# Around each inner LayerNorm: a hand-written order on four engines, transposes among the output matmuls, next weights split ahead, a ring of six

## The chip, the cores and the metric

The kernel runs on one core of a Trainium2 chip. Its time is the device time of one launch in microseconds (us); the kernel before takes 1643.83 us, the median of three runs (1643.48 to 1646.4). Five engines work side by side, each on its own list of instructions: TensorE (PE) multiplies, VectorE (DVE) and ScalarE (ACT) work element by element, GpSimd (POOL) does a few small things, and SyncE (SP) issues the weight transfers. They wait for each other by semaphores.

## What is computed

Two layers on 256 tokens of width 1024. In each, with a = 4^(1/4):

```
x <- LN1(a*x + 1/2 * (silu(x Wg) * (x Wu)) Wo)      first FFN, inner width 4096
x <- LN2(a*x + M(x))                                 the mixer
x <- LN3(a*x + 1/2 * (silu(x Wg') * (x Wu')) Wo')    second FFN
```

M(x) projects x once, runs three mixers on parts of it (gated DeltaNet, chunk attention with a relative bias, sliding-window attention with sinks), projects each back to 1024, weights the three with sigmoid gates of x, adds them (the merge), and multiplies by an output matrix. LN is a LayerNorm over the 1024 channels with gain and bias. All is float32.

## The kernel before

The 256 tokens are two row tiles of 128, called t = 0 and t = 1. Every product is done in three matmuls on split operands: a weight `raw` becomes `hi` (a rounded copy, by ACT, L90) and `lo` (raw minus hi, by DVE or POOL, L91); the activations x are split the same way into `xhl` (hi by ACT at L142, lo by DVE at L144). Then hi·hi, hi·lo and lo·hi are summed in PSUM. Weights come in chunks of 1 MB through SP's queue into three `raw` buffers; the halves go into rings of five `hi` and five `lo` buffers, and some chunks into other tiles that are free at the time.

An FFN runs over 32 column units u. Unit u multiplies x by one chunk (gate and up columns), and the output matrix is added up in blocks of two units. The last six units' output matmuls are done by `finish` (L222), row tile by row tile, and behind each row tile comes `norm` (L311): per half of 512 channels, x plus the PSUM sum (L317) and its statistics (L318), then mean and variance (L320, L322), the reciprocal root on POOL (L324), times gain (L326), plus bias (L335). Then PE transposes the eight 128x128 blocks of the row tile (L338) into PSUM, and ACT and DVE split them into `xhl` in two groups of four (L142, L144). The first three units of an FFN that follows a LayerNorm, and the first projection of the mixer (324 columns, twice), are multiplied with x as the stationary operand, so that row tile 0 can start before row tile 1 is normalized (L301 to L303, and `rows`, L220); the gated rows of those three units are transposed one by one (L270).

The mixer starts with four chunks of that first projection, then goes through a fixed list of projections, gates and branches (ORDER). Branches end with a merge on DVE (L602, L605), a split of the merged tiles (L142, L146), the output matrix through `finish`, and LN2. In the branches and the output matrix the program puts part of the `lo` splits on POOL; so it does for four of the six splits of an FFN's first three units (PFF).

The order of instructions on each engine is worked out before the run by a scheduler that simulates the program (`schedule_with_timeline_sim=True`), not by the order in the source. Weight transfers leave SP in the order in which the scheduler puts them. LayerNorm gains and biases are loaded through POOL's queue (`load_ln`), those of the first FFN of layer 0 through SP's.

There are six LayerNorms: LN1, LN2 and LN3 in each layer. The last one only writes the result. In the profiled execution LN1 of layer 0 lies at about 255 to 292 us from the span's start, LN2 at 532 to 578 and LN3 at 812 to 850; in layer 1 LN1 lies at 1070 to 1108 and LN2 at 1348 to 1394.

## Time and profile before

| | |
|---|---|
| median of three runs | 1643.83 us |
| the profiled execution | 1646.21 us, of which the span 1644.5 us |
| mean granted TensorE clock | 0.997 |
| PE busy | 1620.9 us |
| DVE / ACT / POOL busy | 1045.7 / 791.5 / 175.3 us |
| PE waiting, as the list of waits has it | for the merge 3.4 us, for mixer scores 3.1 us, for split x 1.5 + 1.1 + 0.8 us |

The table is read from the slowest (here the only) core. Busy time of PE is modelled from the starts of pipelined matmuls: the record of a 256-column matmul reads 0.28 us, though the next starts 0.12 us after it, so gaps are read from starts, and durations of PE records are not added up.

### The profile page before, as it was taken

To read this page: it belongs to the slowest core of one execution; us is meant where nothing else is said; L and a number is where in the kernel's file an instruction comes from. 1 tells how busy PE (TensorE), PEld (TensorE's weight loads), DVE (VectorE), ACT (ScalarE), POOL (GpSimd) and SP (SyncE) were. 2 spreads that over 40 slices of the span, in tenths; PEclk is the share of its full clock that TensorE was granted. 3 is DMA by queue.
4 is the path that set the end of the run, shared out by engine and by line. 5 is a ranking of instruction groups with operands and counts; after the bars stand their busy time and mean duration, and the time that the engine had idled before them with its cause. 6 is when DMAs were issued, how large, how long until landed. Compare 5 with 4: busy or idle time off the path is not lost.

```text
span 1644.5 us, 29265 instructions
## 1 busy us (share of the span) xinstructions
PE 1620.9 (99%) x12238; PEld 1511.0 (92%) x12238; DVE 1045.7 (64%) x1580; ACT 791.5 (48%) x1297; POOL 175.3 (11%) x145
## 2 busy tenths in 40 slices
PE   8999999999999999999999999999999999999998
PEld 7999998999889899999899999989988889999997
DVE  6555556889669755555655555667986696555555
ACT  5444453665444444444444444536744444544442
POOL 0000002123014400000110000011320053000000
PEclk9999999999999999999999999999999999999999
DMA  8655553634335555555555555535353355555552
GB/s 295 248 203 184 202 208 113 226 138 156 129 127 198 182 204 183 203 184 201 186 198 184 201 187 198 209 140 203 134 167 118 108 191 193 206 185 199 187 198 78
DMA packets 52341, 298.28 MB, mean 181 GB/s; under 512 B 11600, under 2 KB 13520, under 8 KB 18672
## 3 DMA queue, kind: packets, MB, share of 16 engines
q1 hardware_dynamic: 50208, 289.39, 49.2%
q0 software_dynamic: 2000, 7.01, 1.3%
q8 instruction: 96, 1.57, 0.4%
q14 instruction: 37, 0.30, 0.1%
HBM read 294.94 MB, written 1.44 MB: 180 GB/s over the span
## 4 chain that ended last, share of the span: by engine, by line
PE 93%; DVE 4%; ACT 1%; DMA 1%; issue 0%; SPq 0%; POOL 0%; DVEq 0%; ACTq 0%; POOLq 0%
PE mm L189 37%; PE sm L189 20%; PE acc L204 16%; PE acc L220 8%; DVE lo L91 2%; PE acc L192 1%; PE acc L301 1%; PE acc L303 1%; PE acc L685 1%; PE sm L515 1%; PE acc L302 1%; PE sm L566 1%; PE sm L507 1%; PE sm L514 1%; ACT hi L90 1%; DVE cv L459 1%
## 5 line engine op out<-in xcount | busy, mean ns | idle before, releaser
L91 DVE TENSOR_TENSOR lo<-raw,hi 128x1024 fp32r<-128x1024 f32 (+1 forms) x498 | 617.3, 1245 | 470.6 <-ACT hi L90 469.9
L90 ACT ACTIVATE hi<-raw 128x1024 fp32r<-128x1024 f32 (+1 forms) x542 | 564.2, 1050 | 645.9 <-PE mm L189 196.9
L189 PE MATMUL mm<-xhl,hi 128*128 128x256 f32 x3488 | 618.1, 280 | 0.0
L189 PEld LDWEIGHTS mm<-xhl,hi 128*128 128x128 f32 x3488 | 533.2, 189 | 8.9 <-issue 5.8
L189 PE MATMUL mm<-xhl,lo 128*128 128x256 f32 x1744 | 486.5, 279 | 0.0
L189 PE MATMUL sm<-xhl,hi 128*128 128x256 f32 x1952 | 338.7, 277 | 0.8 <-ACT hi L90 0.8
L189 PEld LDWEIGHTS mm<-xhl,lo 128*128 128x128 f32 x1744 | 329.6, 189 | 4.3 <-issue 2.4
L189 PEld LDWEIGHTS sm<-xhl,hi 128*128 128x128 f32 x1952 | 296.1, 188 | 3.0 <-ACT hi L90 1.0
L189 PE MATMUL sm<-xhl,lo 128*128 128x256 f32 x976 | 270.0, 277 | 0.8 <-DVE lo L91 0.8
L204 PE MATMUL acc<-hi,g 128*128 128x512 f32 x728 | 200.4, 391 | 0.0
L189 PEld LDWEIGHTS sm<-xhl,lo 128*128 128x128 f32 x976 | 183.4, 188 | 2.0 <-DVE lo L91 1.0
L204 PEld LDWEIGHTS acc<-hi,g 128*128 128x128 f32 x728 | 132.4, 188 | 24.2
L91 POOL TENSOR_TENSOR lo<-raw,hi 128x1024 fp32r<-128x1024 f32 (+1 forms) x44 | 104.0, 2377 | 367.5 <-DVE g L144 241.2
L204 PE MATMUL acc<-lo,g 128*128 128x512 f32 x416 | 128.4, 390 | 0.0
L204 PEld LDWEIGHTS acc<-lo,g 128*128 128x128 f32 x416 | 78.1, 188 | 16.8
L324 POOL TENSOR_TENSOR rs<-ve,nh 128x1 f32<-128x1 f32 x12 | 11.8, 985 | 764.6 <-DVE ve L322 764.6
L220 PE MATMUL acc<-hi,g 128*128 128x512 f32 x320 | 92.8, 392 | 0.0
L220 PEld LDWEIGHTS acc<-hi,g 128*128 128x128 f32 x320 | 59.3, 188 | 13.3 <-ACT g L142 0.8
L220 PE MATMUL acc<-lo,g 128*128 128x512 f32 x160 | 54.7, 391 | 0.0
L144 DVE TENSOR_TENSOR g<-th,g 128x256 fp32r<-128x256 f32 x119 | 51.0, 429 | 2.1 <-ACT g L142 1.9
L142 ACT ACTIVATE g<-th 128x256 fp32r<-128x256 f32 x119 | 47.7, 401 | 6.4 <-DVE th L243 6.4
L459 DVE SCALAR_TENSOR_TENSOR cv<-cin,par,cv 128x256 f32<-128x256 f32 x72 | 41.7, 624 | 0.2
(231 smaller groups left out, 1538.2 us busy)
## 6 DMA issues: line engine op xcount, KB each, us to landing
raw<-w2i SPq DMA_DIRECT2D x64, 1024.0 KB, 4.8
raw<-w1i SPq DMA_DIRECT2D x62, 1024.0 KB, 4.8
raw<-w1o SPq DMA_DIRECT2D x32, 1024.0 KB, 4.8
raw<-w2o SPq DMA_DIRECT2D x32, 1024.0 KB, 4.9
raw<-wg SPq DMA_DIRECT2D x28, 1024.0 KB, 4.8
raw<-wgt SPq DMA_DIRECT2D x24, 1024.0 KB, 4.8
raw<-wbr SPq DMA_DIRECT2D x12, 1024.0 KB, 4.8
raw<-wout SPq DMA_DIRECT2D x8, 1024.0 KB, 4.8
```

Source lines behind the costliest of these rows:

```text
L90: nc.scalar.activation(out=hi, in_=raw, func=AF.Copy)
L91: (eng or nc.vector).tensor_tensor(out=lo, in0=raw, in1=hi.bitcast(F32), op=ALU.subtract)
L142: nc.scalar.activation(out=hi, in_=src, func=AF.Copy, scale=scale)
L144: nc.vector.tensor_tensor(out=lo, in0=src, in1=hi.bitcast(F32), op=ALU.subtract)
L189: self.nc.tensor.matmul(out, w, x, start=start, stop=stop)
L192: self.nc.tensor.matmul(*h[:3], start=h[3], stop=False)
L204: self.nc.tensor.matmul(o, x, y, start=st, stop=False)
L220: mm(acc[h], x[:, c], y[:, h * n:h * n + n], start=start and i == 0, stop=stop and i == 2)
L301: mm(out, xh, wh, start=start, stop=False)
L302: mm(out, xh, wl, start=False, stop=False)
L303: mm(out, xl, wh, start=False, stop=stop)
L459: V.scalar_tensor_tensor(out=cv, in0=cin[:, q:q + S], scalar=w[:, q:q + 1], in1=cv, op0=ALU.mult, op1=ALU.add)
```

## The change

`finish` no longer ends with one `norm` per row tile. `norm` is cut into `norm_a` (everything up to the bias) and `norm_b` (transposes and split of x). From the start of `finish` until the next stage's first part is done, the four engines PE, DVE, ACT and POOL take their instructions in the order of the source (`manual_schedule`); the rest is left to the scheduler as before. Two new classes hold the head of the next stage and are called from `finish` at four places: `before` any output matmul, `amid` (behind row tile 0), `between` (in row tile 1, ahead of its last two units), `behind` all. There they load and split the first weights of the next stage.

The transposes of row tile 0 now come after the first three of the last twelve output matmuls of row tile 1, and nine follow them. The transposes of row tile 1 come in the next stage: in an FFN after three of the eight steps of unit 2 of row tile 0, in the mixer after seven of the eight steps of row tile 0. In an FFN the transposes of the gated rows are gathered and done behind the next unit. Of the six weight splits of an FFN's first three units, one is now on POOL and five on DVE.

The rings of `hi` and `lo` have six buffers in place of five. Gains and biases are loaded through SP's queue (in an FFN at unit 10, in the mixer behind the last output chunk), and so are the mixer's small tables `par` and `row`, ahead of the first chunk. The number of matmuls and transposes is the same.

On PE at LN1 of layer 0 the order was this (L220 is an output matmul of row tile 1 where it reads g, and the mixer's first projection where it reads xhl; L338 is a transpose):

```order
L220 MATMUL acc<-lo,g 128x512
L220 MATMUL acc<-hi,g 128x512 x2
L220 MATMUL acc<-lo,g 128x512
L220 MATMUL acc<-hi,g 128x512 x2
L220 MATMUL acc<-lo,g 128x512
L220 MATMUL acc<-hi,g 128x512
L338 MATMUL sm<-con,x 128x128 x8
L220 MATMUL acc<-hi,xhl 128x324 x2
```

and now is this (L350 stands for L220, L473 for L338):

```order
L350 MATMUL acc<-lo,g 128x512
L350 MATMUL acc<-hi,g 128x512
L473 MATMUL sm<-con,x 128x128 x8
L350 MATMUL acc<-hi,g 128x512
L350 MATMUL acc<-lo,g 128x512
L350 MATMUL acc<-hi,g 128x512 x2
L350 MATMUL acc<-lo,g 128x512
L350 MATMUL acc<-hi,g 128x512 x2
L350 MATMUL acc<-lo,g 128x512
L350 MATMUL acc<-hi,g 128x512
L350 MATMUL acc<-hi,xhl 128x324 x2
```

Nine output matmuls of 512 columns now stand between row tile 0's transposes and the first matmul that reads its split. (Numbers of a line differ between the two because lines were added above.)

On DVE ahead of LN2 of layer 0, with L602 and L605 the merge, L146 the lo of a merged tile, and L317 the start of the LayerNorm on row tile 0, the order was this:

```order
L602 SCALAR_TENSOR_TENSOR g_5450<-g_5450,mm_5952 128x512
L146 SCALAR_TENSOR_TENSOR g_6015<-g_3451,g_6015 128x256
L605 TENSOR_TENSOR g_4184<-g_4184,g_5450 128x512
L146 SCALAR_TENSOR_TENSOR g_6018<-g_4184,g_6018 128x256
L602 SCALAR_TENSOR_TENSOR g_5581<-g_5581,mm_5979 128x512
L146 SCALAR_TENSOR_TENSOR g_6021<-g_4184,g_6021 128x256
L605 TENSOR_TENSOR g_3890<-g_3890,g_5581 128x512
L146 SCALAR_TENSOR_TENSOR g_6024<-g_3890,g_6024 128x256
L146 SCALAR_TENSOR_TENSOR g_6027<-g_3890,g_6027 128x256
L317 SCALAR_TENSOR_TENSOR x_73<-acc_6033,x_73 128x512
```

and now is this (L727, L730, L276 and L449 stand for L602, L605, L146 and L317; L97 is the lo of a weight, here of unit 0 of the next FFN):

```order
L727 SCALAR_TENSOR_TENSOR g_5453<-g_5453,mm_5955 128x512
L276 SCALAR_TENSOR_TENSOR g_6018<-g_3454,g_6018 128x256
L730 TENSOR_TENSOR g_4187<-g_4187,g_5453 128x512
L97 TENSOR_TENSOR lo_6086<-raw_6082,hi_6084 128x1024
L276 SCALAR_TENSOR_TENSOR g_6021<-g_4187,g_6021 128x256
L276 SCALAR_TENSOR_TENSOR g_6024<-g_4187,g_6024 128x256
L727 SCALAR_TENSOR_TENSOR g_5584<-g_5584,mm_5982 128x512
L730 TENSOR_TENSOR g_3893<-g_3893,g_5584 128x512
L97 TENSOR_TENSOR lo_6090<-raw_6082,hi_6088 128x1024
L276 SCALAR_TENSOR_TENSOR g_6027<-g_3893,g_6027 128x256
L276 SCALAR_TENSOR_TENSOR g_6030<-g_3893,g_6030 128x256
L449 SCALAR_TENSOR_TENSOR x_73<-acc_6033,x_73 128x512
```

Two lo splits of the next FFN's first chunk have come in among the merge. The halves that the output matmuls read (g_6021 to g_6030) stand behind them.

On DVE from the LayerNorm of row tile 1 into the next FFN, at LN3 of layer 0, the order was this (L91 is the lo of a weight, L144 of split x, L243 the gated product of one unit):

```order
L91 TENSOR_TENSOR lo_9216<-raw_9213,hi_9215 128x1024
L320 BN_AGGR mv_8958<-st_8953 128x2
L144 TENSOR_TENSOR xhl_72<-sm_8902,xhl_72 128x4x128
L144 TENSOR_TENSOR xhl_72<-sm_8910,xhl_72 128x4x128
L322 TENSOR_SCALAR ve_8960<-mv_8958 128x1
L326 SCALAR_TENSOR_TENSOR x_73<-x_73,mv_8958,kq_6231 128x512 x2
L335 SCALAR_TENSOR_TENSOR x_73<-x_73,rs_8962,kq_6231 128x512 x2
L243 TENSOR_TENSOR th_9045<-cv_9046,acc_8995 128x128
L144 TENSOR_TENSOR xhl_72<-sm_8967,xhl_72 128x4x128
L243 TENSOR_TENSOR th_9077<-cv_9078,acc_9007 128x128
L144 TENSOR_TENSOR xhl_72<-sm_8975,xhl_72 128x4x128
```

and now is this, from the ve row on (L454, L458, L463 are L322, L326, L335; L382 is L243; L97 is L91; L274 is L144):

```order
L454 TENSOR_SCALAR ve_8996<-mv_8994 128x1
L458 SCALAR_TENSOR_TENSOR x_73<-x_73,mv_8994,kq_7075 128x512 x2
L463 SCALAR_TENSOR_TENSOR x_73<-x_73,rs_8998,kq_7075 128x512 x2
L382 TENSOR_TENSOR th_9034<-cv_9035,acc_9004 128x128
L97 TENSOR_TENSOR lo_9038<-raw_8955,hi_8959 128x1024
L97 TENSOR_TENSOR lo_9219<-raw_9215,hi_9217 128x1024
L97 TENSOR_TENSOR lo_9223<-raw_9215,hi_9221 128x1024
L382 TENSOR_TENSOR th_9064<-cv_9065,acc_9005 128x128
L274 TENSOR_TENSOR xhl_72<-sm_9077,xhl_72 128x4x128
L274 TENSOR_TENSOR xhl_72<-sm_9084,xhl_72 128x4x128
```

Three lo splits (the second half of unit 2, and both halves of unit 3) now stand behind the LayerNorm and ahead of row tile 1's split of x.

The diff, cut to its core:

```diff
...
+FOUR = {mybir.EngineType.PE, mybir.EngineType.DVE, mybir.EngineType.Activation, mybir.EngineType.Pool}
...
+class FfnHead:
...
+        self.tags = (OTHER if wide else (RING, RING)) + (RING if wide else OTHER[0], RING if wide else OTHER[1]) + (RING, RING)
...
+    def before(self):
+        self.load(0)
+        if self.wide:
+            self.load(1)
+    def amid(self):
+        if not self.wide:
+            self.load(1)
+    def between(self):
+        r = self.b.ring
+        self.raw = r.load(self.wi[2])
+        self.hi = [r.high(self.raw[:, j * 1024:j * 1024 + 1024], 1024, RING) for j in range(2)]
+        self.ws.append([r.low(self.hi[0], self.raw[:, 0:1024], 1024, RING, self.b.nc.gpsimd)])
...
+    def turn(self):
+        b = self.b
+        todo, self.todo = self.todo, []
+        for gg, t, u in todo:
+            c = slice(t * 128, t * 128 + 128)
+            tp = b.ps([128, 128], "sm")
+            b.nc.tensor.transpose(tp, gg, b.ident)
+            b.split(self.g[u][:, 0, c], self.g[u][:, 1, c], tp)
+    def units(self):
+        b = self.b
+        self.ps = [b.ps([128, 2, S], "acc" if u < 2 else "mm") for u in range(3)]
+        self.g = [b.tl([128, 2, S], "g", F32R) for u in range(3)]
+        self.unit(0, 0, range(8))
+        self.gate(0, 0)
+        self.ws[2].append(b.ring.low(self.hi[1], self.raw[:, 1024:], 1024, RING))
+        self.unit(0, 1, range(8))
+        self.gate(0, 1)
+        self.unit(0, 2, range(3))
+        b.norm_b(1)
+        self.unit(0, 2, range(3, 8))
+        self.turn()
+        self.gate(0, 2)
+        self.unit(1, 0, range(8))
+        self.turn()
+        self.gate(1, 0)
+        self.unit(1, 1, range(8))
+        self.turn()
+        self.gate(1, 1)
+        self.unit(1, 2, range(8))
+        self.turn()
+        b.region.__exit__(None, None, None)
+        self.gate(1, 2)
+        return [(t[:, 0], t[:, 1]) for t in self.g]
...
+class MixHead:
...
+    def before(self):
+        b, sync = self.b, self.b.nc.sync
+        self.par = b.tl([128, NPAR], "par")
+        sync.dma_start(out=self.par, in_=b.a["par"][self.l])
+        self.row = b.tl([128, NROW], "row")
+        sync.dma_start(out=self.row, in_=b.a["row"][self.l].partition_broadcast(128))
+        self.load(0)
+        self.load(1)
+    def amid(self):
+        pass
+    def between(self):
+        self.load(2)
+    def behind(self):
+        self.load(3)
+    def units(self, pg):
+        b = self.b
+        def part(t, k):
+            b.rows(pg[t], t, (b.xh[:, k], b.xl[:, k]), self.ws[k], k == 0, k == 7)
+        for k in range(7):
+            part(0, k)
+        b.norm_b(1)
+        part(0, 7)
+        for k in range(8):
+            part(1, k)
+        b.region.__exit__(None, None, None)
...
-    def finish(self, acc, gs, ws, scale, gb, last, start=False):
+    def finish(self, acc, gs, ws, scale, gb, nxt, start=False):
         n = len(ws)
+        if nxt is None:
+            for t in range(2):
+                for h in range(2):
+                    for i in range(n):
+                        self.rows(acc[t], t, gs[i], ws[i], start and i == 0, i == n - 1, (h,))
+                self.norm_a(t, acc[t], scale, gb, True)
+            return
+        self.region = self.tc.manual_schedule(engines=FOUR)
+        self.region.__enter__()
+        nxt.before()
         for t in range(2):
-            tail = n if last else TAIL
-            for i in range(n - tail):
+            for i in range(n - TAIL):
                 self.rows(acc[t], t, gs[i], ws[i], start and i == 0, False)
+                if t == 1 and i == n - TAIL - 1:
+                    nxt.between()
             for h in range(2):
-                for i in range(n - tail, n):
+                for i in range(n - TAIL, n):
                     self.rows(acc[t], t, gs[i], ws[i], False, i == n - 1, (h,))
-            self.norm(t, acc[t], scale, gb, last)
-
...
+                    if t == 1 and h == 0 and i == n - TAIL:
+                        self.norm_b(0)
+            self.norm_a(t, acc[t], scale, gb, False)
+            if t == 0:
+                nxt.amid()
+        nxt.behind()
...
+            if u in (6, 10):
...
+                    if u == 10:
+                        lng = self.load_ln(lnp, nc.sync)
+                    elif head is None:
...
+            if head is not None and u == n0:
+                with self.tc.issue_after(head.last.ins):
+                    self.wide(ps, w, self.xs[0], self.xs[1], 8)
+                    head.turn()
+            else:
+                self.wide(ps, w, self.xs[0], self.xs[1], 8)
+            self.gate(gg, ps[:, 0], ps[:, 1])
...
-    def norm(self, t, acc, scale, gb, last):
+    def norm_a(self, t, acc, scale, gb, last):
...
+    def norm_b(self, t):
+        q = slice(t * 128, t * 128 + 128)
+        for h in range(2):
             tp = self.ps([128, 4, 128], "sm")
             for k in range(4):
-                nc.tensor.transpose(tp[:, k], y[:, h * 512 + k * 128:h * 512 + k * 128 + 128], self.ident)
+                o = h * 512 + k * 128
+                self.nc.tensor.transpose(tp[:, k], self.x[:, t, o:o + 128], self.ident)
...
-        gb = self.load_ln(a["ln"][l, 1])
...
+        with self.tc.issue_after(ring.last.ins):
+            gb = self.load_ln(a["ln"][l, 1], nc.sync)
...
-BUFS = dict(raw=3, hi=5, lo=5, g=12, dec=2, eg=2, cin=2, cv=2, th=2, sq=2, s=2, pT=2, qk=2, vv=2, lev=1, nd=2,
+BUFS = dict(raw=3, hi=6, lo=6, g=12, dec=2, eg=2, cin=2, cv=2, th=2, sq=2, s=2, pT=2, qk=2, vv=2, lev=1, nd=2,
...
```

## Rows read from the trace of the kernel before

**Rows 1.** The page's busy times: us, share of the span, instructions.

```profile
PE 1620.9 (99%) x12238; PEld 1511.0 (92%) x12238; DVE 1045.7 (64%) x1580; ACT 791.5 (48%) x1297; POOL 175.3 (11%) x145
```

**Rows 2.** Stretches: from:to, length, busy time of each engine, TensorE's granted clock, DMA.

```profile
core 0: us, PE busy (x) PEld busy (x) DVE busy (x) ACT busy (x) POOL busy (x), PEclk, DMA share, GB/s
...
255.00:292.00 37.00, 36.26 (x214) 32.64 (x214) 22.56 (x36) 11.20 (x17) 8.23 (x6) 1.00 0.34 120
292.00:532.00 240.00, 236.18 (x2018) 219.94 (x2017) 191.27 (x372) 132.97 (x284) 53.76 (x49) 0.99 0.45 157
532.00:578.00 46.00, 45.87 (x282) 40.26 (x281) 33.00 (x52) 20.27 (x33) 18.96 (x12) 1.00 0.54 198
...
812.00:850.00 38.00, 36.15 (x251) 33.27 (x250) 24.47 (x42) 14.29 (x25) 11.13 (x7) 1.00 0.43 148
```

**Rows 3.** PE's waits by line and releaser: us in total, times, longest.

```profile
PE sm L514 <- DVE qk L581: 3.1, 2, 1.6
...
PE acc L220 <- ACT xhl L142: 1.5, 4, 0.5
```

**Rows 4.** Timeline, PE at the first LayerNorm: start, us, instruction, [idle before <-releaser].

```profile
271.83 0.39 PE L220 MATMUL acc<-hi,g 128*128 128x512 f32 x1
272.06 1.03 PE L338 MATMUL sm<-con,x 128*128 128x128 f32 x8
273.58 0.57 PE L220 MATMUL acc<-hi,xhl 128*128 128x324 f32 x2 [0.49 <-ACT xhl L142]
...
281.34 0.56 PE L220 MATMUL acc<-hi,xhl 128*128 128x324 f32 x2 [0.25 <-ACT xhl L142]
```

**Rows 5.** Timeline, PE at the LayerNorm after the second FFN.

```profile
822.35 0.39 PE L301 MATMUL acc<-hi,xhl 128*128 128x256 f32 x1 [1.08 <-ACT xhl L142]
...
824.09 0.39 PE L303 MATMUL acc<-hi,xhl 128*128 128x256 f32 x1 [0.77 <-DVE xhl L144]
824.31 0.28 PE L301 MATMUL acc<-hi,xhl 128*128 128x256 f32 x1
824.43 0.28 PE L302 MATMUL acc<-lo,xhl 128*128 128x256 f32 x1
```

**Rows 6.** Timeline, ACT at the same LayerNorm.

```profile
821.72 1.07 ACT L142 ACTIVATE xhl<-sm 128x512 fp32r<-128x512 f32 x2
```

**Rows 7.** Timeline, DVE at the LayerNorm after the second FFN.

```profile
815.82 1.41 DVE L335 SCALAR_TENSOR_TENSOR x<-x,rs,kq 128x512 f32<-128x512 f32 x2
...
821.84 1.52 DVE L91 TENSOR_TENSOR lo<-raw,hi 128x1024 fp32r<-128x1024 f32 x1
...
823.40 1.23 DVE L144 TENSOR_TENSOR xhl<-sm,xhl 128x512 fp32r<-128x512 f32 x2
...
824.62 2.19 DVE L326 SCALAR_TENSOR_TENSOR x<-x,mv,kq 128x512 f32<-128x512 f32 x2
826.73 1.41 DVE L335 SCALAR_TENSOR_TENSOR x<-x,rs,kq 128x512 f32<-128x512 f32 x2
```

**Rows 8.** Timeline, DVE ahead of the mixer's LayerNorm.

```profile
517.41 1.22 DVE L91 TENSOR_TENSOR lo<-raw,hi 128x1024 fp32r<-128x1024 f32 x1
...
521.97 3.42 DVE L91 TENSOR_TENSOR lo<-raw,hi 128x1024 fp32r<-128x1024 f32 x1
...
536.24 2.05 DVE L146 SCALAR_TENSOR_TENSOR g<-g 128x256 fp32r<-128x256 f32 x1 [0.48 <-ACT g L142]
...
540.37 0.76 DVE L146 SCALAR_TENSOR_TENSOR g<-g 128x256 fp32r<-128x256 f32 x2 [0.54 <-ACT g L142]
```

**Rows 9.** Timeline, POOL in the same stretch.

```profile
532.79 5.22 POOL L91 TENSOR_TENSOR lo<-raw,hi 128x1024 fp32r<-128x1024 f32 x2 [2.34 <-ACT hi L90]
```

**Rows 10.** Timeline, PE at the mixer's longest stall.

```profile
391.12 0.48 PE L514 MATMUL sm<-kc,qk 64*128 64x128 f32 x2 [1.59 <-DVE qk L581]
```

**Rows 11.** Stretches around that stall, columns as in rows 2.

```profile
389.00:392.50 3.50, 1.91 (x13) 1.38 (x12) 3.47 (x12) 2.73 (x4) 0.20 (x2) 0.99 0.64 255
392.50:396.00 3.50, 3.50 (x19) 3.50 (x19) 3.40 (x11) 0.00 (x0) 0.00 (x0) 0.52 0.00 0
```

More of the change, by code (lines that the diff above doesn't have):

```diff
@@ new lines, with __init__, load, behind @@
+class MixHead:
+    def __init__(self, b, l):
+        self.b, self.l, self.w = b, l, b.a["wg1"][l]
+        self.tags = OTHER + (RING,) * 6
+        self.ws = []
+    def load(self, j):
+        self.ws += self.b.ring.chunk(self.w[j], 2 * NG1, NG1, self.tags[2 * j:2 * j + 2], self.b.engs(PG1[2 * j:2 * j + 2]))
+    def before(self):
[7 more added lines that the diff above has]
+    def amid(self):
+        pass
+    def between(self):
+        self.load(2)
+    def behind(self):
+        self.load(3)
+    def units(self, pg):
+        b = self.b
+        def part(t, k):
[7 more added lines that the diff above has]
+        b.region.__exit__(None, None, None)
@@ L254, in ffn @@
         else:
[L255 to L272 removed]
+            n0 = NFIRST
+            g = head.units()
         for u in range(n0, 32):
             w = self.ring.chunk(wi[u])
[L275 removed]
+            if u in (6, 10):
                 with self.tc.issue_after(self.ring.last.ins):
[L277 removed]
+                    if u == 10:
+                        lng = self.load_ln(lnp, nc.sync)
+                    elif head is None:
                         self.second()
[L279 to L280 removed]
             gg = self.tl([128, S], "th")
             ps = self.ps([128, 2, S], ("mm", "sm")[u // 2 % 2])
[L283 to L284 removed]
+            if head is not None and u == n0:
[5 more added lines that the diff above has]
+            self.gate(gg, ps[:, 0], ps[:, 1])
             t = self.tl([128, 2, S], "g", F32R)
@@ L302, in mm3r @@
         mm(out, xh, wl, start=False, stop=False)
-        mm(out, xl, wh, start=False, stop=stop)
+        return mm(out, xl, wh, start=False, stop=stop)
     def load_ln(self, lnp, q=None):
@@ L347, in exp8, with mixer @@
         self.nc.gpsimd.tensor_tensor(out=out, in0=self.en.rearrange("p (t h) -> p t h", t=2), in1=in_, op=ALU.pow)
-    def mixer(self, l):
+    def mixer(self, l, head, nxt):
         nc, a = self.nc, self.a
@@ L353, in mixer @@
         xh, xl = self.xh, self.xl
-        par = tl([128, NPAR], "par")
-        q0 = nc.sync if l == 0 else G
-        q0.dma_start(out=par, in_=a["par"][l])
-        row = tl([128, NROW], "row")
-        q0.dma_start(out=row, in_=a["row"][l].partition_broadcast(128))
+        par, row = head.par, head.row
+        b2 = par[:, P_B2:P_B2 + NG2]
+        pg = [[ps([128, 324], "acc") for h in range(2)] for t in range(2)]
+        head.units(pg)
         hbg = tl([128, 24], "hbg")
         V.tensor_scalar(out=hbg, in0=par[:, P_BG:P_BG + 24], scalar1=0.5, scalar2=None, op0=ALU.mult)
-        b2 = par[:, P_B2:P_B2 + NG2]
-        pg = [[ps([128, 324], "acc") for h in range(2)] for t in range(2)]
-        ws = []
-        tags = OTHER + (RING,) * 6
-        for j in range(4):
-            ws += ring.chunk(a["wg1"][l, j], 2 * NG1, NG1, tags[2 * j:2 * j + 2], self.engs(PG1[2 * j:2 * j + 2]))
-        for t, k in [(0, k) for k in range(7)] + [(1, 0), (0, 7)] + [(1, k) for k in range(1, 8)]:
-            self.rows(pg[t], t, (xh[:, k], xl[:, k]), ws[k], k == 0, k == 7)
         g1 = tl([128, 2, NG1], "g1")
@@ L538, in head_b @@
             s = tl([128, 384], "s")
-            (q0 if h == 0 else G).dma_start(out=s, in_=a["rb"][l, h])
+            (nc.sync if l == 0 and h == 0 else G).dma_start(out=s, in_=a["rb"][l, h])
             sc = scores(qk[:, 0], qk[:, 1])
@@ L844, in emit @@
         b = Build(nc, tc, Pool(sb, BUFS), Pool(pp, PSUM), dr, a)
+        head = None
         for l in range(L):
-            b.ffn(a["w1i"][l], a["w1o"][l], a["ln"][l, 0], l == 0, False)
-            b.mixer(l)
-            b.ffn(a["w2i"][l], a["w2o"][l], a["ln"][l, 2], False, l == L - 1)
+            mix = MixHead(b, l)
+            mid = FfnHead(b, a["w2i"][l], False)
+            end = FfnHead(b, a["w1i"][l + 1], True) if l < L - 1 else None
+            b.ffn(a["w1i"][l], a["w1o"][l], a["ln"][l, 0], head, mix)
+            b.mixer(l, mix, mid)
+            b.ffn(a["w2i"][l], a["w2o"][l], a["ln"][l, 2], mid, end)
+            head = end
 def _layout(v):
```

94 lines of the change are left out of this document (44 added, 50 removed).

## Prediction, on record before the changed kernel ran

> **What bounds the kernel now.** I read the page first: PE is busy in 1620.9 of 1644.5 us [rows 1], so the others matter only where PE waits for them. The view by stretches says where that is, as length minus PE busy. Its rows for layer 0 [rows 2] give 0.74 us at LN1 (37.00 − 36.26), 0.13 at LN2, 1.85 at LN3, and 3.82 inside the mixer. The change is about the LayerNorms, so what it can win there is small by this view. The list of PE's waits [rows 3] puts 1.5 us in four pieces on ACT's split of x in the mixer's first projection (two LN1s, two waits each), and 3.1 us in two pieces on the query of the fifth score product in the mixer.
>
> The timelines show the waits. At LN1 PE does the last output matmul, eight transposes, and then stands 0.49 us until ACT has split the first half; row tile 1 costs another 0.25 [rows 4]. At LN3 it stands 1.08 us for ACT and 0.77 for DVE [rows 5]. There ACT ends its two halves at 821.72 + 1.07, and DVE begins its own only at 823.40, behind a lo split of 1.52 us [rows 6, 7].
>
> **The change part by part.** *Transposes of row tile 0 among the output matmuls.* They need the normalized row tile. At LN3 it is ready at 815.82 + 1.41 = 817.2 us [rows 7], and the new place is nine matmuls and the transposes ahead of 821.27, where PE ran dry (822.35 − 1.08 [rows 5]). A 512-column matmul takes 0.23 us from start to start (271.83 to 272.06 [rows 4]), so the place is at 821.27 − 1.03 − 2.07 = 818.2: the data is there. Nine matmuls are 2.07 us of work, against 1.07 us for ACT and 1.23 for DVE, which run after each other by halves. So the wait goes, provided ACT and DVE do nothing else then. Removed: 0.74 at each LN1 and 1.85 at LN3. To each of the six waits I add 0.16 us, because a matmul behind a wait does not overlap the one ahead of it: 0.28 long against 0.12 from start to start (824.31, 824.43 [rows 5]). That is 2 × (0.74 + 0.32) + 1.85 + 0.32 = 4.3 us.
>
> *The FFN heads, row tile 1.* Here something is given back. At LN3 PE reaches the FFN at 821.27 without waiting. 24 + 24 + 9 matmuls of 0.12 us bring it to 828.1, where row tile 1's transposes stand. Its x was ready at 826.73 + 1.41 = 828.14; without the lo split (1.52) and the x split (1.23) ahead of it [rows 7], and with the accumulation ending later by the 1.03 us of transposes, that becomes about 826.4. PE does not wait there. DVE then has three lo splits, 3 × 1.22 us [rows 8], and two small products ahead of row tile 1's x split, so the first half of xl is there at about 826.4 + 3.7 + 0.5 + 0.6 = 831.2. PE needs it after the transposes (1.03), 15 matmuls (1.8), two gate transposes (0.26) and two more matmuls: 831.4. It is a tie. But in before the gain step (L326) took 2.19 us for two where the bias step took 1.41 [rows 7], and POOL keeps one lo split at this place; the same 0.8 us later makes PE wait 0.8 us. With both ends 0 and 1.6 (two such collisions), I take 0.8. At the two LN2 heads the same chain stands, with an idle of only 0.13 to win [rows 2]; I take 0.3 net each, from 0 to 0.8.
>
> *Ahead of LN2.* Two lo splits of the next FFN's first chunk are put among the merge on DVE, ahead of halves that the output matmuls read. Undisturbed they cost 2 × 1.22 = 2.44 us; the chain there has 0.48 + 0.54 = 1.02 us in which DVE waited for ACT [rows 8]. PE idles 0.13 us in that whole stretch [rows 2], so some slack lies between DVE and PE; how much the trace does not say. The bounds are 0 (all in slack) and 3.4 us per layer (one split like the 3.42 us one, uncovered). I take 0.5 per layer, near the low end: 2.44 − 1.02 = 1.4 is what the chain grows by, and the slack takes a part of it.
>
> *Ring of six, loads, queues.* The ring only lets a chunk's halves come sooner. Gain, bias and the mixer's tables go through SP's queue between chunks in place of POOL's, so the chunk behind them starts later by their transfer. The DMA engines are 34 to 54% busy in these stretches [rows 2], and the three raw buffers give the cover; I cost both at nothing, with 1 us per LayerNorm to either side as the ends where that cover is thin. The program has 35 lo splits on POOL in place of 44; what this frees or loads on DVE is inside the terms above.
>
> *The mixer.* Its instructions are the same, but the scheduler was run anew, and the fifth score product now stands eight matmuls later. This is a rival, below; in the sum it is nothing.
>
> The sum: −4.3 + 0.8 + 0.6 + 1.0 = −1.9 us. Against the profiled execution's own 1646.21 (span 1644.5 and 1.7 around it) this gives 1644.3; that execution is 2.4 us above the median, and against the median the forecast is 1641.9 us.
>
> **What speaks against it.** During the branches a lo split on DVE took 3.42 us where another took 1.22 [rows 8], and POOL ran pairs of lo splits in these same stretches (5.22 us for two [rows 9]). The Trainium skill, page "SBUF — State Buffer", section "SBUF: two separate sides", says that VectorE and GpSimd share one pair of ports under an exclusive lock, held for the whole instruction, so that the later one fully blocks. The trace agrees: 3.42 less 1.22 is 2.2, most of one POOL split (5.22 / 2 = 2.61). By that rule each lo split put among the merge waits out a POOL split whenever one is under way, and the time comes out as in rival C.
>
> **Rivals.**
>
> A, the forecast: waits at LN1 and LN3 go, 2.4 us come back in the heads and ahead of LN2: 1641.9.
>
> B, faster through the mixer. PE stands 1.59 us for the query at 389.5 [rows 10], and in the 3.5 us behind it the granted clock is 0.52, that is the lower level, 1.2 GHz, after a stretch in which PE was busy in 1.91 of 3.5 us [rows 11]. Half speed for 3.5 us costs 0.48 × 3.5 = 1.7. If eight more matmuls (0.9 us) ahead of the score, and DVE relieved of some collision with POOL, keep that wait short, the slow stretch goes with it: up to 2 × (1.59 + 1.68) = 6.5 us, so 1635.4; with the wait shortened by 0.9 alone, and the clock kept, about 1636.9. For it: DVE's delay there comes through operations that POOL slowed. Against: the scheduler's clock, not the chip's, decided the new order; and the rest of the mixer can move the other way.
>
> C, slower, ahead of LN2. POOL still does the output matrix's splits there, and one of the two new splits takes 3.42 us and stands uncovered, in each layer. In place of 1.0 us for both layers it costs 2 × 3.43 = 6.9: −4.3 + 0.8 + 0.6 + 6.9 = +4.0, so 1647.8. It turns the sign from 1.45 us per layer, and passes the 0.2% mark at about 3.1. For it: the rows just named, and that program order on DVE can't step round a blocked split. Against: PE's idle of 0.13 at LN2 shows slack of unknown size.
>
> D, no difference. The order of the source puts other work ahead of what PE waits for, in every one of the three kinds of head, by about as much as it won (4.3 us over five heads is 0.9 each; one collision is 0.8): about 1643.8. In this case the waits of before are gone, and new ones of the same sum stand at row tile 1's split. For it: the tie of 831.2 and 831.4 above leaves no room. Against: at LN1 nothing of DVE's new work stands ahead of PE.
>
> **How the numbers follow.** A has 0.45, B 0.25, C 0.17, D 0.13. A's own range is −1.9 with its terms' ends: 1639.5 to 1645. To hold 8 in 10 the range goes from B's full size to C: 1635.5 to 1648. A measurement tells some 0.2% from no change, 3.3 us, so the marks are 1640.5 and 1647.1. Faster: B (0.25) and the lower end of A (0.15), 0.40. Slower: the upper part of C (0.11) and what could go wrong away from these places, which I spread over A, B and D (0.06), 0.17. Same: the rest, 0.43.
>
> **What would show it.** In the stretch view of the changed kernel PE's idle at the LN1s falls to 0.1 or so, at LN3 from 1.85 to about 0.8. In PE's timeline nine output matmuls follow the eight transposes, and the first matmul on split x comes without a gap. New waits of a few tenths stand at the first gate transposes of a head and at row tile 1's first lo·hi matmul, released by DVE. Ahead of LN2 PE waits for DVE's L276 by half a us. B is right if the wait for the fifth score is gone and the clock reads 1.00 behind it; C if a lo split of 2 us or more stands among the merge with a PE wait behind it. I am wrong in the sum if stretches away from the LayerNorms, the mixer's inside above all, change by more than 1 us each without that wait changing; and wrong in the mechanism if PE still waits for row tile 0's split.

## The result, and the profile after

The changed kernel takes 1664.32 us, the median of four runs (1662.3 to 1666.68), against 1644.55 for the kernel before: a ratio of 1.012, with a 95% interval of 1.0099 to 1.014. It is slower by 20 us where 2 us less was forecast, and outside the range. The profiled execution took 1666.12 us, its span 1664.4.

The page of the changed kernel, first line of its busy times, against [rows 1]:

```profile
PE 1629.1 (98%) x12238; PEld 1518.9 (91%) x12238; DVE 1051.7 (63%) x1589; ACT 792.9 (48%) x1297; POOL 142.5 (9%) x124
```

PE's busy time grew by 8 us, although it runs the same 12238 matmuls; the rest of the 20 us is idle. The stretch view, with the columns of [rows 2] and the same bounds (the later stretches have moved a little against the work):

```profile
255.00:292.00 37.00, 35.69 (x215) 32.58 (x214) 25.23 (x36) 12.45 (x17) 8.77 (x6) 1.00 0.32 112
292.00:532.00 240.00, 232.80 (x1938) 215.29 (x1936) 178.85 (x359) 127.87 (x275) 45.23 (x45) 0.96 0.42 146
532.00:578.00 46.00, 42.31 (x255) 38.10 (x256) 37.81 (x51) 19.00 (x27) 14.57 (x7) 0.96 0.46 168
...
812.00:850.00 38.00, 37.44 (x253) 34.16 (x252) 25.36 (x44) 12.71 (x23) 4.21 (x3) 1.00 0.41 152
```

At LN3 PE's idle fell from 1.85 to 0.56 us (38.00 − 37.44), where about 0.8 was forecast. At LN1 it grew from 0.74 to 1.31, where the forecast had 0.1. In the mixer it grew from 3.82 to 7.20, at LN2 (a stretch that now holds the end of the mixer's last branch too) from 0.13 to 3.69, and in both the granted clock is down to 0.96. The list of PE's waits, to be held against [rows 3]:

```profile
PE sm L639 <- DVE qk L706: 8.4, 2, 4.2
PE mm L319 <- DVE g L727: 7.6, 4, 3.6
PE acc L810 <- ACT eg L846: 2.9, 2, 2.5
PE sm L473 <- DVE x L463: 2.6, 2, 1.3
PE sm L171 <- DVE xhl L274: 1.7, 6, 0.3
```

The wait for the fifth score (L514 is now L639) grew from 3.1 to 8.4 us. The wait for the merge in branch R0, the projection of the first mixer's output back to 1024 (L602, now L727), grew from 3.4 to 7.6. One for ACT in the inverse, a step inside the gated DeltaNet (L810), is new, and so is one for row tile 1's normalized x at LN1 (L473). Only the last wait, at the gate transposes (L171), is one that the prediction had.

The time is best placed by a table of PE's own progress: from the last output matmul ahead of one LayerNorm to the last one ahead of the next, from the starts of PE's records in each trace, in us.

| from, to | before | after | e1 | e3 | e5 | e6 | e11 |
|---|---|---|---|---|---|---|---|
| first matmul, LN1 | 270.3 | 270.5 | 267.9 | 269.9 | 270.3 | 270.8 | 271.0 |
| LN1, LN2 (mixer, layer 0) | 283.1 | 296.6 | 296.5 | 282.1 | 282.2 | 285.3 | 277.7 |
| LN2, LN3 (second FFN) | 265.1 | 265.9 | 267.1 | 264.9 | 265.9 | 265.9 | 265.9 |
| LN3, LN1 (first FFN, layer 1) | 267.9 | 266.1 | 270.5 | 269.7 | 265.9 | 266.1 | 265.9 |
| LN1, LN2 (mixer, layer 1) | 283.1 | 290.7 | 289.4 | 283.7 | 282.4 | 279.7 | 277.8 |
| LN2, end of the output matmuls | 265.1 | 265.0 | 267.2 | 264.9 | 265.0 | 265.0 | 265.0 |

(e1 to e11 are the experiments below. In the kernels with the hand order eight transposes, 0.9 us, stand ahead of these bounds where they stood behind them; in rows with a LayerNorm of that kind at both ends this cancels, and it makes the first row 0.9 longer and the last 0.9 shorter. Each column is one profiled execution; those of e5 and e6 lie 2.3 us below and 2.7 us above their kernels' medians.) Of the 20.2 us that the changed kernel lost by this table, 13.5 and 7.6 lie between LN1 and LN2, in the mixers.

**Where the mixer lost it.** The first place is the wait for the fifth score. The query (L706) reads neither the root nor the decay product of the rows below; it stands behind operations on them in DVE's list, and is late when they are. POOL in the changed kernel (L478 a reciprocal root, L97 a lo split, L817 the decay product), and then DVE (L760 the first operation on that root, L706 the query):

```profile
372.30 3.97 POOL L478 TENSOR_TENSOR r<-t,nh 128x16 f32<-128x16 f32 x1 [1.23 <-DVE t L754]
376.25 2.46 POOL L97 TENSOR_TENSOR lo<-raw,hi 128x1024 fp32r<-128x1024 f32 x1
382.28 2.28 POOL L817 TENSOR_TENSOR eg<-nn,con 128x512 f32<-128x512 f32 x1 [3.57 <-DVE nn L779]
```

```profile
376.37 2.37 DVE L760 TENSOR_TENSOR cf<-be,r 128x8 f32<-128x8 f32 x1
...
392.64 0.87 DVE L706 TENSOR_SCALAR qk<-mm,par 128x256 f32<-128x256 f32 x2
```

And the same first operation in the kernel before:

```profile
371.88 0.16 DVE L635 TENSOR_TENSOR cf<-be,r 128x8 f32<-128x8 f32 x1
```

It works on 8 columns, takes 0.16 us in one and 2.37 in the other, and ends at 378.74, just as POOL's split does (376.25 + 2.46 = 378.71). In the kernel before that split stood behind the decay product; POOL's root came 3.8 us earlier there too (at 368.52). The late root alone does not make the wait: in e4 below it comes at 371.67, without a split behind it, and PE waits 1.46 us. So PE stands four microseconds for the query, and runs at half clock behind it. PE's row, and the stretches of the stall (389.00), behind it (393.20, 396.70), behind the wait in the inverse (427.50, the third place below) and behind the one in R0 (542.60), with the columns of rows 2:

```profile
393.18 0.79 PE L639 MATMUL sm<-kc,qk 64*128 64x128 f32 x2 [4.21 <-DVE qk L706]
```

```profile
389.00:393.20 4.20, 0.02 (x1) 0.02 (x1) 3.61 (x11) 2.35 (x4) 0.20 (x2) 0.88 0.79 265
393.20:396.70 3.50, 3.50 (x13) 2.85 (x14) 3.50 (x8) 0.38 (x1) 0.00 (x0) 0.50 0.25 49
396.70:400.00 3.30, 3.30 (x21) 3.30 (x21) 2.38 (x10) 2.23 (x6) 0.00 (x0) 0.65 1.01 395
...
427.50:436.50 9.00, 9.00 (x83) 7.57 (x80) 5.00 (x12) 2.81 (x9) 0.63 (x1) 0.50 0.42 140
...
542.60:545.80 3.20, 3.16 (x15) 3.16 (x16) 2.70 (x3) 1.01 (x3) 1.60 (x1) 0.50 0.24 97
```

PE was busy 0.02 of 4.2 us, and the next 3.5 run at 0.50, the lower of its two levels, the 3.3 behind at 0.65. In the kernel before it was 0.52 over 3.5 us [rows 11].

The second place is R0. POOL, DVE (L276 the lo of a merged tile, L727 the merge that frees the PSUM buffer of R0's last product) and PE (L350 the first output matmuls, L319 R0's last product):

```profile
534.01 10.20 POOL L97 TENSOR_TENSOR lo<-raw,hi 128x1024 fp32r<-128x1024 f32 x4 [3.63 <-ACT hi L92]
```

```profile
537.45 4.54 DVE L276 SCALAR_TENSOR_TENSOR g<-g 128x256 fp32r<-128x256 f32 x2 [0.48 <-ACT g L272]
541.91 0.68 DVE L727 SCALAR_TENSOR_TENSOR g<-g,mm 128x512 f32<-128x512 f32 x1
```

```profile
538.51 0.63 PE L350 MATMUL acc<-lo,g 128*128 128x512 f32 x2
542.64 0.79 PE L319 MATMUL mm<-kq,hi 128*128 128x256 f32 x2 [3.51 <-DVE g L727]
```

Four POOL splits in a row take 10.20 us; beside them two small lo operations take 4.54, where two undisturbed ones took 0.76 [rows 8]. PE has done four output matmuls (the last two at 538.51), comes to R0's last product, and waits 3.51 us for a buffer. In the kernel before R0's last product stood ahead of all output matmuls.

The third place is the inverse, in layer 0:

```profile
427.03 1.97 PE L810 MATMUL acc<-sq,eg 64*64 64x64 f32 x32 [2.47 <-ACT eg L846]
```

Behind this wait the granted clock is 0.50 for nine us, the row from 427.50 above. In e8 below PE has the same matmuls in the same order and waits 2.41 us here, but the clock is 1.00 from 424.0 to 437.0. From L810 to the first matmul behind 436.5, PE took 9.55 us in the changed kernel and 5.34 in e8, so the half clock cost 4.2 us. In layer 1 this wait is 0.43 us and no such stretch follows; wait and clock together are the larger part of the 5.9 us by which layer 0 lost more than layer 1. The four times of the changed kernel lie in two pairs (1662.3 and 1662.52, 1666.12 and 1666.68). A slow stretch here in two of the four executions would fit, but only one of them has a trace, so that is not shown.

### The profile page after: what moved, and what is told of

Read it like the earlier page. It is cut to its first block, busy times and chain, and to the rows that moved or that the text cites. A ratio compares the mean times of both kernels' runs of the same rounds, so it can differ in the third digit from the quotient of the medians.

```text
span 1664.4 us, 29333 instructions
## 1 busy us (share of the span) xinstructions
PE 1629.1 (98%) x12238; PEld 1518.9 (91%) x12238; DVE 1051.7 (63%) x1589; ACT 792.9 (48%) x1297; POOL 142.5 (9%) x124
## 4 chain that ended last, share of the span: by engine, by line
PE 86%; DVE 9%; DMA 2%; ACT 2%; issue 1%; POOL 0%; SPq 0%; DVEq 0%; ACTq 0%; POOLq 0%
PE mm L319 34%; PE sm L319 20%; PE acc L334 16%; PE acc L350 7%; DVE lo L97 2%; PE acc L322 1%; DVE x L463 1%; DVE g L730 1%; PE sm L640 1%; PE acc L810 1%; DVE cv L584 1%; DVE xhl L274 1%; PE sm L639 1%; PE sm L632 1%; DMA d<-nb 1%
## 5 line engine op out<-in xcount | busy, mean ns | idle before, releaser
L97 DVE TENSOR_TENSOR lo<-raw,hi 128x1024 fp32r<-128x1024 f32 x507 | 617.7, 1225 | 477.3 <-ACT hi L92 473.4
L319 PE MATMUL mm<-xhl,hi 128*128 128x256 f32 x3488 | 617.1, 279 | 0.0
L319 PEld LDWEIGHTS mm<-xhl,hi 128*128 128x128 f32 x3488 | 533.9, 189 | 7.0 <-issue 3.7
L319 PE MATMUL mm<-xhl,lo 128*128 128x256 f32 x1744 | 487.4, 279 | 0.0
L319 PE MATMUL sm<-xhl,hi 128*128 128x256 f32 x1952 | 338.3, 276 | 0.8 <-ACT hi L92 0.8
L319 PEld LDWEIGHTS mm<-xhl,lo 128*128 128x128 f32 x1744 | 329.7, 189 | 4.4 <-issue 3.0
L319 PEld LDWEIGHTS sm<-xhl,hi 128*128 128x128 f32 x1952 | 295.9, 188 | 3.3 <-ACT hi L92 1.0
L319 PE MATMUL sm<-xhl,lo 128*128 128x256 f32 x976 | 269.6, 276 | 0.8 <-DVE lo L97 0.8
L319 PEld LDWEIGHTS sm<-xhl,lo 128*128 128x128 f32 x976 | 183.2, 188 | 2.0 <-DVE lo L97 1.0
L350 PE MATMUL acc<-hi,g 128*128 128x512 f32 x320 | 93.1, 391 | 0.0
L97 POOL TENSOR_TENSOR lo<-raw,hi 128x1024 fp32r<-128x1024 f32 (+1 forms) x35 | 82.0, 2355 | 92.3 <-ACT hi L92 92.3
L350 PEld LDWEIGHTS acc<-hi,g 128*128 128x128 f32 x320 | 59.6, 188 | 11.8
L350 PE MATMUL acc<-lo,g 128*128 128x512 f32 x160 | 54.5, 389 | 0.0
L274 DVE TENSOR_TENSOR g<-th,g 128x256 fp32r<-128x256 f32 x119 | 49.9, 419 | 2.6 <-ACT g L272 2.4
```

The source lines that it names most:

```text
L97: (eng or self.nc.vector).tensor_tensor(out=lo, in0=raw, in1=hi.bitcast(F32), op=ALU.subtract)
L274: nc.vector.tensor_tensor(out=lo, in0=src, in1=hi.bitcast(F32), op=ALU.subtract)
L319: self.nc.tensor.matmul(out, w, x, start=start, stop=stop)
L350: mm(acc[h], x[:, c], y[:, h * n:h * n + n], start=start and i == 0, stop=stop and i == 2)
```

## The experiments

Theory R after the comparison: the ring of six, not the hand order, lost the time, because the scheduler, given a buffer more, put POOL's splits and the first output matmuls earlier in the mixer. Its rival H: program order on the four engines around the LayerNorms is what costs. The ring alone already changes the lists that the scheduler makes. POOL's list in the mixer of the kernel before, and of the same kernel with a ring of six:

```
L344 TENSOR_TENSOR r_3940<-t_3935,nh 128x16
L453 MEMSET cin 128x3 x2
L692 TENSOR_TENSOR eg<-nn,con 128x512
L677 TENSOR_TENSOR lev<-nn,con 128x512
L91 TENSOR_TENSOR lo<-raw,hi 128x1024 x2
```

```
L453 MEMSET cin 128x3 x2
L344 TENSOR_TENSOR r_3940<-t_3935,nh 128x16
L91 TENSOR_TENSOR lo<-raw,hi 128x1024
L692 TENSOR_TENSOR eg<-nn,con 128x512
L677 TENSOR_TENSOR lev<-nn,con 128x512
L91 TENSOR_TENSOR lo<-raw,hi 128x1024
```

One lo split has come ahead of eg, the decay product, and the root r has gone behind two small fills.

**e1, the ring alone.**

```diff
-BUFS = dict(raw=3, hi=5, lo=5,
+BUFS = dict(raw=3, hi=6, lo=6,
...
-    nc = _bacc.Bacc("TRN2", target_bir_lowering=False, num_devices=1)
+    nc = _bacc.Bacc("TRN2", target_bir_lowering=False, num_devices=1, dynamic_dma_scratch_size=8192)
```

> The kernel before with rings of six in place of five (and the smaller scratch for DMA descriptors that makes room for them), nothing else. Theory R (ring): with six buffers the scheduler puts one POOL lo split ahead of the decay product in the mixer, and the first output matmuls ahead of branch R0's last product; these two, not the LayerNorms, are where the changed kernel lost its time. Then this kernel shows a wait of about 4.2 us (before 1.6) for the fifth score in each layer and one of about 3.5 us at R0's last product, the stretches around the LayerNorms stay as before, and the time is 1656 to 1665 us. Theory H (hand order): program order on four engines around the LayerNorms is what costs. Then the time is within 3 us of 1644.5.

Measured: 1672.16 us (1668.1 to 1674.95), ratio 1.0162 (1.0141 to 1.0184). Its waits:

```profile
PE sm L514 <- DVE qk L581: 8.6, 2, 4.3
PE mm L189 <- DVE g L602: 8.5, 5, 3.8
PE acc L303 <- DVE xhl L144: 5.7, 3, 2.4
```

The ring alone loses more than the whole change does, and 7 us more than the upper end of theory R. Both waits of theory R are there, 4.3 and 3.8 us at the longest. One thing was not expected: PE also waits 5.7 us in three pieces for the lo of x (L144) at the FFN heads, so the stretches around LN2 and LN3 did not stay as before; the three FFN rows of the table are 2.0, 2.6 and 2.1 us longer. The edit also takes the changed kernel's smaller scratch for DMA descriptors. That is not the cause: e3 and e5 keep it and take 1645.84 and 1645.56 us.

**e2, the changed kernel without the hand order.**

```diff
-        self.region = self.tc.manual_schedule(engines=FOUR)
+        self.region = contextlib.nullcontext()
```

> The changed kernel with the hand order taken away: the same source, rings of six, but the scheduler orders all engines everywhere. Theory R: the two waits in the mixer (about 4.2 and 3.5 us per layer) stay, and the time is 1656 to 1667 us. Theory H: the time falls to 1643 to 1647 us.

Measured: 1667.26 us, one run. The waits, in the same order as those of e1:

```profile
PE sm L640 <- DVE qk L707: 8.5, 2, 4.3
PE mm L319 <- DVE g L728: 7.6, 4, 3.6
```

H falls: without the hand order the time is no better, and lies 0.3 us above the upper end of theory R.

**e3, neither the hand order nor the ring of six** (e2's edit, and `hi=5, lo=5`).

> The changed kernel with neither the hand order nor the ring of six: next weights split ahead, transposes in the source's places, loads through SP, the scheduler's order. Theory R: the wait for the fifth score is about 1.6 us again, the one at R0's last product is gone, and the time is 1641 to 1647 us. A third theory S, that the loads and splits ahead cost by themselves (DVE beside POOL ahead of the mixer's LayerNorm): 1650 us or more.

Measured: 1645.84 us (1643.72 to 1648.05), ratio 1.0002 (0.9992 to 1.0011). The waits for the score and in R0 are 1.6 and 1.5 us at the longest, as in the kernel before (1.6 and 1.7). Splits and loads ahead, by themselves, cost nothing that can be measured; theory S falls.

**e4, no gate splits on POOL.**

```diff
-PGT = ("vv", "vv", "vg")
+PGT = ("vv", "vv", "vv")
```

> The changed kernel with all gate splits of branch 2 on DVE, none on POOL (four fewer on POOL in each layer). Theory R, its POOL part: the wait for the fifth score falls from 4.2 to 1.6 us or less since no POOL split stands ahead of the decay product, the wait at R0's last product stays at about 3.5, and the time is 1653 to 1660 us. Rival: DVE's own queue is what delays the query, four more splits of 1.2 us make it no better, and the time stays at 1662 to 1668 us.

Measured: 1649.44 us, one run, better than the theory's 1653 to 1660.

```profile
PE mm L319 <- DVE g L727: 6.4, 5, 3.7
PE sm L639 <- DVE qk L706: 2.9, 2, 1.5
...
PE acc L810 <- ACT eg L846: 1.6, 2, 0.8
```

The wait for the score fell from 8.4 to 2.9 us in all, though DVE got four more splits per layer. The first operation on the root takes 0.15 us again (0.16 in the kernel before). The edit also put the score three matmuls earlier in PE's list. At R0 the wait of layer 1 is still 3.66 us, as the theory said; that of layer 0 fell from 3.51 to 1.79, which it did not say. Nor did it say that the one in the inverse would fall, from 2.9 to 1.6 in all, with the clock at 1.00 behind it in layer 0. That gain of clock is 4.2 us, about what the run came out below the theory.

**e5, the hand order on a ring of five.** The hand order holds six pairs at once where a head's first chunk meets four output halves; with five it would wait for itself, so the plain ring of five was not tried. A pair of buffers of its own for the heads takes the sixth's place, and the mixer's scheduling sees a ring of five.

```diff
-        self.tags = (OTHER if wide else (RING, RING)) + (RING if wide else OTHER[0], RING if wide else OTHER[1]) + (RING, RING)
+        self.tags = (OTHER + (RING, PAIR) if wide else (RING, PAIR) + OTHER) + (RING, RING)
...
-        self.tags = OTHER + (RING,) * 6
+        self.tags = OTHER + (RING, PAIR) + (RING,) * 4
...
-BUFS = dict(raw=3, hi=6, lo=6,
+BUFS = dict(raw=3, hi=5, lo=5, hx=1, lx=1,
```

> The changed kernel with rings of five, and one more hi/lo pair that only the heads of the next stage use (without a sixth buffer somewhere the hand order can't hold its halves). The mixer sees a ring of five, as before the change. Theory R (ring): the waits for the fifth score (4.2) and at R0's last product (3.5) fall back to 1.6 and to 1.7 or less, and what is left is the hand order alone. From the trace of the changed kernel that is -1.75 us at LN3, +0.4 at each LN1, +0.8 at each FFN head behind LN2, about +0.7 in all: 1642 to 1647 us. If the hand order costs in other ways (theory H), it stays above 1650.

Measured: 1645.56 us (1643.26 to 1649.08), ratio 1.0002 (0.9993 to 1.0012).

```profile
PE sm L640 <- DVE qk L707: 3.2, 2, 1.6
PE mm L320 <- DVE g L728: 3.0, 2, 1.5
PE acc L351 <- DVE g L277: 2.7, 2, 1.4
PE sm L474 <- DVE x L464: 2.6, 2, 1.3
```

The loss is gone with the ring, so R stands: the mixer takes 282.2 and 282.4 us. But the hand order alone is worth nothing that can be measured either. LN3 to LN1 gains 1.9 us (267.86 to 265.92); what it gives back is the wait for row tile 1 at LN1 (L474, 1.3 each), 0.8 behind each LN2, and a new wait of 1.4 per layer for a merged tile's lo (L351 on L277).

**e6, all mixer splits on DVE, ring of six kept.** The edit is e4's, with `PBR = ("vv", "vv", "vv")` and `PWO = "vvvvvvvv"` (branches and output matrix).

> The changed kernel, ring of six, with all lo splits of gates, branches and output matrix on DVE, none on POOL. The scheduler then puts R0's last product ahead of all output matmuls by itself. Theory R with POOL collisions as its means: the wait for the fifth score is 1.5 us or less, the one at R0's last product is gone, 1639 to 1646 us. Rival: DVE has too much to do in the mixer (some twelve splits of 1.2 us more per layer), new waits for DVE's lo stand in the branches, and the time is 1650 us or more.

Measured: 1641.79 us (1638.65 to 1647.4), ratio 0.9983 (0.9968 to 0.9997). As the theory had it: the wait for the score is 1.46 us, the one at R0 is gone from the list. The wait in the inverse is not a matter of POOL's splits in gates, branches and output matrix, since this kernel has none there and still waits 2.52 us in layer 0, with the clock at 0.50 for nine us behind it (from 422.0). It goes with the ring: e1, e2 and e8 have 2.4 us as well, e3, e5, e10 and e11 have no such wait. What makes it short in e4 and e9 (0.8) stays open.

**e7, the same edit on the kernel before.**

> The kernel before with the same edit: all lo splits of gates, branches and output matrix on DVE. If collisions of DVE with POOL make the waits of before too (1.6 us for the fifth score, 1.7 in R0), both fall below 1 us, the half-clock stretch behind the score goes with it, and the time is 1635 to 1641 us. Rival (DVE's load decides): 1645 us or more.

Measured: 1650.95 us (1646.89 to 1654.53), ratio 1.003 (1.0017 to 1.0042). A miss in the time, and half a miss for the theory that POOL's splits make the waits of before:

```profile
PE sm L514 <- DVE qk L581: 4.3, 2, 2.2
PE acc L301 <- ACT xhl L142: 3.1, 3, 1.1
...
PE mm L189 <- DVE g L602: 0.5, 2, 0.3
```

The wait in R0 fell from 3.4 to 0.5 us in all, as the theory had it. But the wait for the score grew (3.1 to 4.3), and at the FFN heads PE waits three times for hi of split x and three times for lo, where it waited once for each. So the edit that gains on the changed kernel loses on this one; what makes the heads late here was not tried further.

**e8, only the output matrix's splits on DVE** (`PWO = "vvvvvvvv"`). PE's order is that of the changed kernel.

> The changed kernel with only the output matrix's six splits per layer moved from POOL to DVE. PE's order is the same as in the changed kernel, word for word; R0's last product still stands behind the first output matmuls. If POOL's splits make the merge late: the wait there falls from 3.5 to 1 us or less in each layer, with the half-clock stretch behind it, and the time is 1652 to 1659 us; the wait for the fifth score stays at 4.2. Rival, that the product's place alone makes the wait: it stays above 2.5 us, and the time is 1661 to 1668.

Measured: 1652.72 us, one run.

```profile
PE acc L350 <- DVE g L276: 2.4, 2, 1.2
```

The wait at R0's last product is gone with PE's order unchanged, which is 4.8 us in layer 0 and 4.9 in layer 1; the wait for the score is 8.4 us, as it was. It was POOL that made the merge late, and not the product's place alone; a wait of 1.2 per layer for a merged tile's lo is left. Another 4.2 us of the difference in the traces is the clock behind the inverse, which this edit does not touch.

**e9, two POOL splits ahead of the root at LN1.** In the changed kernel DVE's bias step for row tile 1 (L463) and POOL beside it, at LN1:

```profile
274.81 1.41 DVE L458 SCALAR_TENSOR_TENSOR x<-x,mv,kq 128x512 f32<-128x512 f32 x2
276.13 4.04 DVE L463 SCALAR_TENSOR_TENSOR x<-x,rs,kq 128x512 f32<-128x512 f32 x2
```

```profile
275.93 3.70 POOL L97 TENSOR_TENSOR lo<-raw,hi 128x648 fp32r<-128x648 f32 x2
```

The gain step takes 1.41 us for its two; the bias step, beside two POOL splits that program order put behind the root, takes 4.04.

```diff
+            if t == 1:
+                nxt.behind()
             self.norm_a(t, acc[t], scale, gb, False)
             if t == 0:
                 nxt.amid()
-        nxt.behind()
```

> The changed kernel with one call moved: the mixer head's last chunk is issued ahead of row tile 1's norm_a, not behind it. On POOL two lo splits of 648 columns then stand ahead of the reciprocal root in place of behind it; no other engine's order changes. If these two splits are what stretched DVE's bias step to 4.04 us for two (1.41 elsewhere) and made PE wait 1.31 us for row tile 1 at each LN1, the step takes under 2 us, that wait is gone in both layers, PE's stretch from LN1 to the mixer shortens by 1.3 to 1.6 us each, and the whole by 2.6 to 3.2. If DVE is late for another reason (the root comes later, so the bias step waits), the wait stays at 1 us or more.

Measured: 1661.12 us, one run. DVE's gain and bias steps then:

```profile
277.13 2.12 DVE L459 SCALAR_TENSOR_TENSOR x<-x,mv,kq 128x512 f32<-128x512 f32 x2
279.17 1.40 DVE L464 SCALAR_TENSOR_TENSOR x<-x,rs,kq 128x512 f32<-128x512 f32 x2
```

The bias step is at 1.40 and PE's wait for it has gone from the list; the gain step grew to 2.12, and both together fell from 5.4 to 3.4 us. The whole is 3.2 us below the changed kernel's median, though the stretch ahead of LN1, which the edit does not touch, took 2.3 us more in this run. The mixer stretches fell by 5.4 us (296.6 to 291.1) and 1.9 (290.7 to 288.8). In layer 0 PE gained 1.5 us at LN1, as forecast, and 5.8 at the inverse: the wait there went from 2.47 to 0.80, and the clock behind it stayed at 1.00. R0 gave 1.4 back. In the changed kernel DVE stood 2.32 and 1.83 us for small transfers through memory ahead of the inverse, here 0.63 and 1.80; why one delay less at LN1 shortens that stays open.

**e10 and e11, the pieces put together:** e5 with the output matrix's splits on DVE (e10), and with e9's order too (e11).

> The hand order with rings of five and the extra pair, and the output matrix's splits on DVE in place of POOL. The run with the pair alone still waited 1.5 us in R0 and 1.4 us for a merged tile's lo, per layer, beside POOL's splits. If these are the collisions with POOL, both fall below 0.5 us and the time is 1638 to 1642 us. If DVE's six more splits per layer take their place, it stays at 1643 to 1648.

> Both of the last two edits on the hand order with rings of five and the pair. If the collisions at LN1 and ahead of LN2 add up: 1636 to 1641 us, faster than the kernel before and than the run without POOL splits. If one of them is only moved: 1642 to 1647.

Measured: e10 1638.19 us, one run; e11 1635.47 us (1635.16 to 1636.49), ratio 0.995 (0.9933 to 0.9967), faster than both kernels and 0.5 us below the range given. In e10 the waits in R0 and for a merged tile's lo are gone, as expected. The two largest waits of e11:

```profile
PE sm L641 <- DVE qk L708: 3.2, 2, 1.6
PE sm L172 <- DVE xhl L275: 1.7, 6, 0.3
```

What it still has is the score's 1.6 us per layer and the 0.3 at the gate transposes. Each mixer takes 5.3 us less than before. About 1.7 of that (an estimate, 0.48 × 3.5 from [rows 11]) is not a shorter wait but the clock: behind the score PE still waits 1.58 us, and the granted clock is then 1.00.

## Why the prediction was wrong

*Transposes among the output matmuls: right.* PE's rows at LN1, against [rows 4]:

```profile
269.26 1.03 PE L473 MATMUL sm<-con,x 128*128 128x128 f32 x8
270.06 0.48 PE L350 MATMUL acc<-hi,g 128*128 128x512 f32 x1
...
271.97 0.39 PE L350 MATMUL acc<-hi,g 128*128 128x512 f32 x1
272.19 0.46 PE L350 MATMUL acc<-hi,xhl 128*128 128x324 f32 x2
...
280.32 0.63 PE L473 MATMUL sm<-con,x 128*128 128x128 f32 x4 [1.31 <-DVE x L463]
```

Eight transposes, nine output matmuls, and the first matmul on split x starts 0.22 us after the last output matmul, without a gap. The waits of 0.49 and, at LN3, 1.08 and 0.77 [rows 5] are gone; LN3 to LN1 shortened by 1.7 us (267.86 to 266.13), where the terms said 2.2 − 0.8 = 1.4.

*The FFN heads: right in kind, the sizes off.* At LN3, against [rows 5] and [rows 7], DVE and then PE:

```profile
840.11 3.49 DVE L97 TENSOR_TENSOR lo<-raw,hi 128x1024 fp32r<-128x1024 f32 x3
...
843.71 1.28 DVE L274 TENSOR_TENSOR xhl<-sm,xhl 128x512 fp32r<-128x512 f32 x2
```

```profile
844.45 0.33 PE L171 MATMUL sm<-con,th 128*128 128x128 f32 x1 [0.29 <-DVE xhl L274]
845.05 0.33 PE L171 MATMUL sm<-con,th 128*128 128x128 f32 x1 [0.27 <-DVE xhl L274]
```

Three lo splits (3.49 us) stand ahead of row tile 1's x split, as the working had it, and that split ends at 844.99. PE waits at the two gate transposes, 0.29 and 0.27 us, because their PSUM buffers are the ones that x split frees: 0.56 in all, where 0.8 was taken. Behind LN2 it is 0.8 us per FFN net, where 0.3 was taken.

*LN1: a term left out.* The working gave 1.06 us of gain at each LN1 and said of DVE's work there that nothing new stands ahead of PE. It had not followed POOL. The mixer head's last two splits went from ahead of the root to behind it, into DVE's bias step. PE waits 1.3 us for that in each layer; e9 shows it, since with the two splits ahead of the root again the wait is gone.

*The mixer: the step that failed.* Of the ring, the loads and the queues it said "I cost both at nothing", with 1 us per LayerNorm to either side. The ring alone costs 26.5 us (1672.16 against 1645.67, e1). I asked only whether a chunk's halves can come sooner on the chip, and not what the scheduler makes of a free buffer. Nor did the ends given for this term enter the range: its upper end for A, 1645, is not the sum of the ends stated. Rival B saw that the fifth score stood eight matmuls later, and read it as relief: more work ahead of a wait. The chance given to it was for the wrong sign. POOL's list, in which one split had passed the decay product, said why the query would come later; of POOL's instructions the prediction took up only the number of lo splits (35 in place of 44).

*Ahead of LN2: rival C's mechanism, in another place.* Two lo splits among the merge were priced at 0.5 us per layer, rival C at 3.4. What came was POOL holding DVE in R0 (4.54 us for two small operations), a wait of 3.5 us and a half-clock stretch. Not the new splits were blocked, but the merge itself; e8 shows it, since moving POOL's six splits away takes the wait off with PE's order unchanged.

*Clock.* That a stall in the mixer is paid twice was right for the changed kernel's trace: each of the three large waits of layer 0 has a stretch at 0.50 behind it. But rival B tied the slow stretch behind the score to the wait, and in e11 they came apart: the wait is still 1.58 us, and the clock behind it 1.00.

## What to carry to other kernels

Where a scheduler sets the order, a buffer more is a change to the order of every engine that shares the ring: compare each engine's list in the stages that the change does not name, POOL's first, before pricing the stages that it does. An engine with small, slow jobs that delays a busy one should do them where nothing waits; here taking six splits per layer from it, and placing two more ahead of a root, brought the hand order from no gain to 8.7 us (1635.47 against 1644.19). And a local win is worth checking against what the same edit releases elsewhere: the hand order by itself measured as nothing until the collisions behind it were moved. And a single run can differ by 4 us from another through the clock behind one stall: look at it before giving the difference to an edit.
